# A hand-written TensorE order for the samples' attention, with pieces of gate products between a unit's parts and their weights issued from ScalarE's queue

## Chip, cores and metric

The kernel runs on one core of a Trainium2 chip. The metric is the device time of one execution in microseconds, taken as the median of several runs. TensorE is called PE, its weight load PEld, VectorE DVE, ScalarE ACT, GpSimd POOL and the sync engine SP. SP issues the DMAs of the kernel before, except for one kind that POOL issues.

## What is computed

One layer of a decoder is computed for a prompt of 512 tokens and for 8 samples of 8 tokens (64 token columns). The part that the change touches is the attention of the samples. It reads the cached latent rows in pages of 128 keys, and carries a running maximum, sum and accumulator over them.

```python
def step(carry, pid):
    m, l, acc = carry
    c = cache_kv_latent[layer, pid]
    kr = cache_k_rope[layer, pid]
    s = scores(c, kr)                       # q_abs . c + q_rope . kr, scaled
    m_new = jnp.maximum(m, jnp.max(s, -1))
    corr = jnp.exp(m - m_new)
    p = jnp.exp(s - m_new[..., None])
    acc = acc * corr[..., None] + jnp.einsum('bhtk,bkl->bhtl', p, c.astype(f32))
    return (m_new, l * corr + jnp.sum(p, -1), acc), None
```

Around it stand products that do not depend on this attention: the two gates `sigmoid(g_a)` and `sigmoid(g_c)`, which are parts of the input projection, the convolution's projection `w_oc`, and, for the prompt's columns, the attention's projection `w_oa`. They merge into `m = sigmoid(g_a) * y_a + sigmoid(g_c) * y_c`, which `w_o` projects. A layer norm and a feed-forward block follow.

## The kernel before

All rows stand transposed, with channels on the partitions and the 576 token columns in two halves of 288. A product is exact to fp32 by a split of both operands into a high and a low part: `mm3` (lines 116 to 119) makes three matmuls of it, named by lines 117, 118 and 119 in the profile. A weight tile comes by `wload` (line 98): a DMA into `wr` (line 107, three buffers), then `split` (line 56): ACT copies the high part to `wh` (line 57), and DVE subtracts it to give `wl` (line 60). `wh` and `wl` have three buffers of 512 columns each.

The program runs in stages: conditioning and first projections; the prompt's attention, with other products merged in; the samples' attention, with the gate products merged in; the output projection with the first norm; the feed-forward block with the second.

The samples' attention has 36 units: for each of 4 pairs of samples one unit of the step's own rows (64 keys) and 8 units of 4 pages for each sample of the pair. `load` (line 556) fetches a unit: SP reads 8 page numbers into registers (line 563) and issues 8 DMAs of 256 KB into `raw` (line 569), and POOL issues 4 indirect DMAs into `kr` (line 573). There are 7 places of `raw`, two to a unit, and 3 of `kr`. `scores` (lines 613 to 633) splits `kr` by ACT (`krh`) and DVE (`krx`, line 625), then multiplies the queries with the latent rows (line 630) and with the rotary rows (line 632). `values` (lines 635 to 680) takes the maximum on DVE (line 646), the exponential on ACT (`S`), transposes `S` on PE (line 653), copies it on ACT (`pT`), multiplies it with the pages on PE (line 661, `pv`), and adds to the accumulator on DVE (line 669). The last unit of a pair also transposes the accumulator (line 676).

The other products are a generator: `fill_gates` (8 tiles of one gate, 8 of `w_oc`, 8 of the other gate) and `fill_oa` (8 tiles of the merged branches). A gate tile is `dense` (line 309): 48 matmuls of 288 columns. `merge` (line 745) draws units of both generators in a ratio. Only SP keeps the written order in this stage. Elsewhere the recording layer's scheduler fixes each engine's order when the program is built, from its own estimate of when things are ready; on the chip every engine then runs its list in that order. As SP keeps the written order, the weights of a tile stand on SP's queue behind the page loads that were written before them, and a page load waits for a place of `raw` to come free.

Of the kernel before, what the change touches and what calls it, by code (L numbers as in the profile page):

```python
# [16 lines left out]
SEQ = 512  # L17
# [8 lines left out]
KVL = 256  # L26
# [17 lines left out]
# column offsets of the per-channel vectors  # L44
# [3 lines left out]
def build(tc, a):  # L48
# [40 lines left out]
    # ---------------------------------------------------------------- base  # L89
# [6 lines left out]
    # weight stream: pool, ring of split tiles, columns of a tile  # L96
    wp = [pool("w", side="right"), 3, 512, 3]

    def wload(src, n=1024, hl=None, tag="", to=None, eng=None):
        """a weight tile and its exact split, as a list of (hi, lo) pieces of wp[2] columns"""  # L100
# [3 lines left out]
        for c in range(0, n, step):  # L104
            m = min(step, n - c)
            raw = wp[0].tile([128, step], F32, tag="wr", bufs=wp[3], name="wr")
            dma(out=raw[:, :m], in_=src[:, c:c + m])
# [31 lines left out]
    def halves(t):  # L139
        """operands of a half-token tile [128, 2, K, HT]"""  # L140
# [8 lines left out]
    def rsqrt(p, vv, out, table=True):  # L149
        """out = 1/sqrt(vv): exp(-ln/2), then one Newton step"""  # L150
# [15 lines left out]
    # right-hand stack: what outlives the attention phases  # L166
# [19 lines left out]
    # ---------------------------------------------------------------- start: ada, h  # L186
# [31 lines left out]
    # weights of the conditioning, in part where results come later  # L218
# [5 lines left out]
    # a quarter of the conditioning gives a quarter of the modulated rows, and those a quarter of the first three tiles  # L224
# [48 lines left out]
    # ---------------------------------------------------------------- latent projections  # L273
    # on the right what the queries end with, on the left what the prompt's attention ends with
# [88 lines left out]
    # values of the prompt, token-major  # L363
# [9 lines left out]
    # new latent rows of the samples, token-major  # L373
# [17 lines left out]
    # ---------------------------------------------------------------- fillers  # L391
# [48 lines left out]

    def fill_gates():
        gc = gates["gc"]
        for j in range(8):
            dense(win(MT["gc"][0] + j), lambda ps, h_, sl: act(gc[:, j, sl], ps))
            yield 1
        act(gc, gc, AF.Sigmoid)
        for j2 in range(4):
            w = wload(a["w_oc"][j2])
# [6 lines left out]
            yield 1  # L455
        ga = gates["ga"] = YP.tile([128, 8, T], F32, tag="y", bufs=1, name="ga")
        for j in range(8):
            dense(win(MT["ga"][0] + j), lambda ps, h_, sl: act(ga[:, j, sl], ps))
            yield 1
        act(ga, ga, AF.Sigmoid)  # L460
        yield 1
# [34 lines left out]
    def prompt_units():  # L496
        for pr in range(4):
# [32 lines left out]
            for kb in range(4):  # L530
                n = SEQ - 128 * kb
                pts = []
                for o in range(2):
# [4 lines left out]
                    pts.append(A2b.tile([128, SEQ], F32, tag="pt", bufs=4, name="pt"))  # L538
                    act(pts[o][:, :n], pt[:, :n])
                # the two heads' columns of the array work side by side  # L540
# [16 lines left out]
    def load(pa, gg):  # L557
        """GP pages of the two batches, and their rotary rows"""
# [18 lines left out]
    def prepare(wk):  # L577
        """the samples' queries against latent rows, and the rotary ones"""
# [5 lines left out]
        # rotary queries against [hi, lo] rows of the first batch, then of the second: block-diagonal  # L584
# [607 lines left out]
```

## Time and profile before

| what | value |
|---|---|
| median of 3 runs | 1171.45 us (1170.65 to 1172.48) |
| span of the profiled execution, first to last instruction | 1174.0 us |
| mean granted PE clock | 0.974 |
| PE busy | 1091.8 us (93%) |
| DVE, ACT, POOL busy | 537.7, 431.7, 225.1 us |
| DMA | 190.07 MB, mean 162 GB/s |
| samples' attention, about 277 to 656 us of the span | 379 us |

Of the profiled execution the profile gives the span and no time beside it; the span lies 2.5 us (0.2%) over the median of the runs. The end of a matmul is modelled and matmuls are pipelined, so a busy PE is not a PE at its peak. What a matmul costs is read from the distance between the starts of matmuls that follow each other.

### The profile page before, as it was taken

Reading aid. Unit: us, or ns where it says so; the run is one execution under the profiler, and the core shown is the slowest. Engines: PE = TensorE matmul, PEld = TensorE weight load, DVE = VectorE, ACT = ScalarE, POOL = GpSimd, SP = SyncE. Lnnn points to the kernel's source line nnn. Section 1 sums busy time; section 2 is a strip of 40 time slices with the busy share of each in tenths; the row PEclk is TensorE's granted clock in tenths of the full one; section 3 lists DMA queues with packets and bytes.
Section 4 is the critical chain, followed back from the end, with each engine's and each line's share of the span. In section 5 each row is a group of like instructions: output and inputs, shape, how many; then the busy total and the mean of one; then the engine's idle time right before and its main releaser. Section 6 shows DMA issues by size and latency. Waiting matters only on the chain.

```text
span 1174.0 us, 19868 instructions
## 1 busy us (share of the span) xinstructions
PE 1091.8 (93%) x7646; PEld 931.6 (79%) x7646; DVE 537.7 (46%) x1059; ACT 431.7 (37%) x859; POOL 225.1 (19%) x232
## 2 busy tenths in 40 slices
PE   6889999998798899989999889899999999999994
PEld 5878787785466466556569889899999999999994
DVE  3476354443132333332247787933233333355656
ACT  2474343435232522332346355332223222334433
POOL 1120000023442342441301421800000000001303
PEclk9999999999799998999999899999999999999998
DMA  9626354418389586696675423032222222455551
GB/s 366 209 96 204 122 185 141 140 46 311 106 294 321 170 300 214 220 310 244 203 239 172 159 73 108 3 107 91 90 72 79 100 75 72 118 178 150 157 181 54
DMA packets 84941, 190.07 MB, mean 162 GB/s; under 512 B 11600, under 2 KB 15568, under 8 KB 84848
## 3 DMA queue, kind: packets, MB, share of 16 engines
q1 hardware_dynamic: 80752, 180.42, 45.8%
q0 software_dynamic: 4096, 8.40, 2.3%
q8 instruction: 60, 0.98, 0.3%
q14 instruction: 33, 0.27, 0.1%
HBM read 185.72 MB, written 3.06 MB: 161 GB/s over the span
## 4 chain that ended last, share of the span: by engine, by line
PE 48%; DVE 7%; DMA 5%; issue 2%; ACT 1%; SPq 1%; POOL 0%; POOLq 0%; ACTq 0%; DVEq 0%
PE acc L117 10%; PE acc L118 9%; PE acc L119 9%; PE sc L117 4%; PE sc L119 4%; PE sc L118 4%; PE sc L630 3%; DMA wr<-in_w_ff_dram 3%; PE pv L661 3%; DVE xr L60 2%; DVE wl L60 2%; ACT wh L57 1%; PE sc L632 1%; SPq L569 1%; DMA raw<-in_page_dram 1%
## 5 line engine op out<-in xcount | busy, mean ns | idle before, releaser
L117 PE MATMUL acc<-h,wl 128*128 128x288 f32 x960 | 288.7, 302 | 14.1 <-DVE wl L60 8.5
L118 PE MATMUL acc<-h,wh 128*128 128x288 f32 x960 | 286.9, 299 | 2.0 <-DVE h L60 1.5
L119 PE MATMUL acc<-h,wh 128*128 128x288 f32 x960 | 284.7, 297 | 1.9 <-issue 1.9
L60 DVE TENSOR_TENSOR wl<-wr,wh 128x512 fp32r<-128x512 f32 (+1 forms) x186 | 178.7, 966 | 212.1 <-ACT wh L57 206.1
L57 ACT ACTIVATE wh<-wr 128x512 fp32r<-128x512 f32 (+2 forms) x196 | 156.6, 807 | 194.5 <-DMA wr<-in_w_ff_dram 58.7
L117 PEld LDWEIGHTS acc<-h,wl 128*128 128x128 f32 x960 | 181.5, 189 | 25.9 <-DVE wl L60 11.2
L118 PEld LDWEIGHTS acc<-h,wh 128*128 128x128 f32 x960 | 182.2, 190 | 7.3 <-issue 5.0
L119 PEld LDWEIGHTS acc<-h,wh 128*128 128x128 f32 x960 | 182.6, 190 | 3.1 <-issue 2.9
L573 POOL DMA_INDIRECT kr<-in_krT_dram,idx x128 | 122.7, 959 | 227.4 <-ACT krh L57 103.0
L117 PE MATMUL sc<-h,wl 128*128 128x288 f32 x336 | 99.9, 297 | 0.0
L118 PE MATMUL sc<-h,wh 128*128 128x288 f32 x336 | 99.4, 296 | 0.0
L119 PE MATMUL sc<-h,wh 128*128 128x288 f32 x336 | 99.1, 295 | 0.0
L630 PE MATMUL sc<-raw,qa 128*64 128x512 f32 x256 | 85.3, 634 | 3.2 <-DMA raw<-in_page_dram 1.8
L60 POOL TENSOR_TENSOR xr<-xr,h 128x288 f32<-128x288 f32 x16 | 17.2, 1098 | 366.1 <-ACT h L57 362.5
L117 PE MATMUL acc<-f,wl 128*128 128x288 f32 x288 | 85.9, 298 | 1.6 <-DVE wl L60 1.6
L118 PE MATMUL acc<-f,wh 128*128 128x288 f32 x288 | 84.9, 295 | 0.0
L119 PE MATMUL acc<-f,wh 128*128 128x288 f32 x288 | 84.7, 294 | 0.0
L661 PE MATMUL pv<-raw,pT 128*64 128x256 f32 x512 | 68.8, 401 | 12.5 <-ACT pT L57 6.3
L661 PEld LDWEIGHTS pv<-raw,pT 128*64 128x64 f32 x512 | 38.5, 143 | 37.7 <-issue 16.0
L119 PEld LDWEIGHTS sc<-h,wh 128*128 128x128 f32 x336 | 63.6, 189 | 0.0
L118 PEld LDWEIGHTS sc<-h,wh 128*128 128x128 f32 x336 | 63.3, 189 | 0.1
L117 PEld LDWEIGHTS sc<-h,wl 128*128 128x128 f32 x336 | 63.2, 188 | 0.1
(326 smaller groups left out, 1767.1 us busy)
## 6 DMA issues: line engine op xcount, KB each, us to landing
raw<-in_page_dram SPq DMA_DIRECT2D x256, 256.0 KB
wr<-in_w_ff_dram SPq DMA_DIRECT2D x76, 512.0 KB
wa<-in_w_ada_dram SPq DMA_DIRECT2D x40, 512.0 KB
wr<-in_w_in_dram SPq DMA_DIRECT2D x64, 256.0 KB
wr<-in_w_ff_dram SPq DMA_DIRECT2D x16, 384.0 KB
wr<-in_w_o_dram SPq DMA_DIRECT2D x18, 256.0 KB
wr<-in_w_oa_dram SPq DMA_DIRECT2D x16, 256.0 KB
x<-in_xT_dram SPq DMA_DIRECT2D x4, 576.0 KB
```

Source lines behind the costliest of these rows:

```text
L57: nc.scalar.activation(out=out, in_=in_, func=func, **kw)
L60: return (eng or v).tensor_tensor(out=out, in0=in0, in1=in1, op=op)
L117: mm(ps, lhsT=wl, rhs=xh, start=start, stop=False)
L118: mm(ps, lhsT=wh, rhs=xl, start=False, stop=False)
L119: mm(ps, lhsT=wh, rhs=xh, start=False, stop=stop)
L569: dma(out=raw[:, j], in_=a["page"][bass.ds(vs[GP * e + j], 1)].rearrange("a p d -> p (a d)"))
L573: g.indirect_dma_start(kr[:, 128 * j:128 * j + 128], None, a["krT"], bass.IndirectOffsetOnAxis(ap=idx[:, i:i + 1], axis=0))
L630: mm(ps[rows(e), :n], lhsT=qa[:, c, 2 * pa + e], rhs=rhs, start=c == 0, stop=False)
L632: mm(ps[:, :n], lhsT=qr[:, i, pa].rearrange("p e q -> p (e q)"), rhs=kx, start=False, stop=i == 0)
L661: mm(pv[rows(e), :KVL], lhsT=pT[:np_, j, e], rhs=rhs, start=j == 0, stop=j == nj - 1)
```

## The change

`values` is cut in three. The maximum, the exponential and the sums move into `scores`; `turn` makes the transposes and `pT`; `values` keeps the products with the pages and the accumulator; `attended` transposes a finished accumulator one unit later. A piece of another product (half a gate tile, one tile of `w_oc` or of `w_oa`) is drawn by `fill` after the values of every unit, and in 8 of the 36 units a second one between the transposes and the scores. PE now keeps the written order in this stage, as SP does. The weights of these pieces are issued from ACT's queue (`wq`), no longer from SP's. In the prompt's attention the two heads' transposes are written in the other order. Comments and descriptions in the code are blank lines now.

```diff
-    def wload(src, n=1024, hl=None, tag="", to=None, eng=None):
+    def wload(src, n=1024, hl=None, tag="", to=None, eng=None, q=None):
...
-            dma(out=raw[:, :m], in_=src[:, c:c + m])
+            (q or dma)(out=raw[:, :m], in_=src[:, c:c + m])
...
+    wq = nc.scalar.dma_start
+
+    def dense_chunks(i, dst):
+        w = wload(a["w_in"][i - 3], q=wq)
+        pss = [ps_acc(), ps_acc()]
+        for p in range(2):
+            gpart(pss, w[p], hs, 0, range(4 * p, 4 * p + 4), 8)
+            if p:
+                for ps, sl in zip(pss, sls):
+                    act(dst[:, sl], ps[:, :HT])
+            yield 1
...
-            dense(win(MT["gc"][0] + j), lambda ps, h_, sl: act(gc[:, j, sl], ps))
-            yield 1
+            yield from dense_chunks(MT["gc"][0] + j, gc[:, j])
...
-                for o in range(2):
+                for o in (1, 0):
                     pt = ps_sc()
...
+            act(S[:, :n], (S if new else ps)[:, :n], AF.Exp, bias=nb[:, g1], scale=SCALE,
                 accum_out=(ll if new else ls)[:, g1])
+            if not new:
+                act(cx[:, g1], mx[:, g0], AF.Exp, bias=nb[:, g1], scale=SCALE)
...
+            return S
...
-            cur, nxt = nxt, scores(*units[i + 1], pages[i + 1]) if i + 1 < len(units) else None
-            values(*u, cur, pages[i])
-            yield 1
+            more = i + 1 < len(units)
+            if more:
+                kx = krn if units[i + 1][1] < 0 else rotary(pages[i + 1])
+            pT = turn(*u, S)
+            fill(2 * i)
+            if more:
+                S = scores(*units[i + 1], pages[i + 1], kx)
+            values(*u, pT, pages[i])
+            fill(2 * i + 1)
+            if u[1] < 0 and u[0] or not more:
+                attended(u[0] - 1 if more else u[0])
...
-            to_m(j, 0, woa(j), gates["a3"])
-            yield 0.25
-        wo.append(wload(a["w_o"][0]))
+            to_m(j, 0, woa(j, q=wq), gates["a3"])
+            yield 1
+        wo.append(wload(a["w_o"][0], q=wq))
...
-        merge(sample_units(A3, qa, qr, pages), F, 21 - PF - P3, 37)
+    A3 = gates["a3"] = pool("a3")
+    extra = 48 - 2 * PF - len(units)
+
+    def fill(s):
+        i = s // 2
+        if s % 2 or (i + 1) * extra // len(units) > i * extra // len(units):
+            next(F, None)
+    with tc.manual_schedule(engines={mybir.EngineType.SP, mybir.EngineType.PE}):
+        sample_stage(A3, qa, qr, pages, fill)
         for _ in F:
             pass
```

On PE, before, this stands in the third pair, where three units follow each other without other work. `raw` are pages, `qa` the queries, `S` the exponentials, `pT` their transposes; L630 and L632 are scores, L653 transposes, L661 values, L117 a gate piece.

```order
L630 MATMUL sc<-raw,qa 64x512
L661 MATMUL pv<-raw,pT 64x256 x8
L630 MATMUL sc<-raw,qa 64x512 x3
L632 MATMUL sc<-krx,qr 128x512 x2
L653 MATMUL sc<-ident,S 128x128 x4
L630 MATMUL sc<-raw,qa 64x512
L661 MATMUL pv<-raw,pT 64x256 x8
L653 MATMUL sc<-ident,S 128x128 x4
L630 MATMUL sc<-raw,qa 64x512 x3
L632 MATMUL sc<-krx,qr 128x512 x2
L661 MATMUL pv<-raw,pT 64x256 x8
L117 MATMUL acc<-h,wl 128x288
```

On PE, after the change, a unit of the first pair reads as follows; L670 is now the transposes, L644 and L646 the scores of the unit after it, L683 the values, and L117 to L119 begin a piece of 24 matmuls.

```order
L119 MATMUL acc<-h,wh 128x288
L670 MATMUL sc<-ident,S 128x128 x4
L644 MATMUL sc<-raw,qa 64x512 x4
L646 MATMUL sc<-krx,qr 128x512 x2
L683 MATMUL pv<-raw,pT 64x256 x8
L117 MATMUL acc<-h,wl 128x288
L118 MATMUL acc<-h,wh 128x288
```

Between a unit's scores and its transposes there now stand the values of the unit before and a whole piece; between its transposes and its values stand the scores of the next unit.

On ACT, before, in the first pair, `krh` is the rotary rows' high part of a later unit, `S,sm` the exponential, `sm` the correction, `gct` a gate tile's copy and `wh` two weight pieces.

```order
L57 ACTIVATE krh<-kr 128x512
L57 ACTIVATE S,sm<-sc,sm 128x512
L57 ACTIVATE sm<-sm 128x1
L57 ACTIVATE wh<-wr 128x512 x2
L57 ACTIVATE pT<-sc 128x512
L57 ACTIVATE krh<-kr 128x512
```

On ACT, after the change, at the same place in the program, the weights' DMAs stand in its list.

```order
L107 DMA wr<-in_w_in_dram 128x512
L57 ACTIVATE krh<-kr 128x512
L57 ACTIVATE S,sm<-sc,sm 128x512
L57 ACTIVATE sm<-sm 128x1
L57 ACTIVATE wh<-wr 128x512
L57 ACTIVATE pT<-sc 128x512
L107 DMA wr<-in_w_in_dram 128x512
```

One weight piece is split in a unit where there were two in every second, and one DMA is issued behind the copy of `pT`.

On SP, before, a gate tile's weights stand between the page loads of two units (L563 reads the page numbers, the ISA rows set an address).

```order
L569 DMA raw<-in_page_dram 128x512
L107 DMA wr<-in_w_in_dram 128x512 x2
L563 TENSOR_LOAD ptab
L569 ISA
L569 DMA raw<-in_page_dram 128x512
```

On SP, after the change, page loads follow page loads.

```order
L579 ISA
L579 DMA raw<-in_page_dram 128x512
L573 TENSOR_LOAD ptab
L579 ISA
L579 DMA raw<-in_page_dram 128x512
```

The two weight DMAs have left the place between them.

More of the change, by code (lines that the diff above doesn't have):

```diff
@@ L454, in fill_gates @@
                     tt(gc[:, j, sl], gc[:, j, sl], ps[:, :HT], MULT)
-            yield 1
+                yield 1
         ga = gates["ga"] = YP.tile([128, 8, T], F32, tag="y", bufs=1, name="ga")
         for j in range(8):
-            dense(win(MT["ga"][0] + j), lambda ps, h_, sl: act(ga[:, j, sl], ps))
-            yield 1
+            yield from dense_chunks(MT["ga"][0] + j, ga[:, j])
         act(ga, ga, AF.Sigmoid)
-        yield 1
     def fill_ada():
@@ L537, in prompt_units @@
                                             Ss[o][:, offs[i] + 128 * kb:offs[i] + 128 * kb + 128], ident)
-                    pts.append(A2b.tile([128, SEQ], F32, tag="pt", bufs=4, name="pt"))
+                    pts[o] = A2b.tile([128, SEQ], F32, tag="pt", bufs=4, name="pt")
                     act(pts[o][:, :n], pt[:, :n])
@@ L604, in prepare, with sample_stage @@
         return qa, qr
-    def sample_units(A3, qa, qr, pages):
+    def sample_stage(A3, qa, qr, pages, fill):
         smask = A3.tile([128, 4, NS], F32, name="smask")
@@ L611, in rows, with rotary, scores @@
             return slice(64 * e, 64 * e + 64)
-        def scores(pa, gg, pages):
+        def rotary(pages):
+            krh = A3.tile([128, GK], F32R, tag="krh", bufs=1, name="krh")
+            kx = A3.tile([128, GK], F32R, tag="krx", bufs=2, name="krx")
+            act(krh, pages["kr"])
+            v.scalar_tensor_tensor(out=kx, in0=krh.bitcast(F32), scalar=nm, in1=pages["kr"], op0=MULT, op1=ADD)
+            return kx
+        def scores(pa, gg, pages, kx):
             ps = ps_sc()
@@ L619, in scores @@
                 smt[pa] = A3.tile([128, 8, NG + 1], F32, tag="sm", bufs=2, name="sm")
-                kx = krn
-            else:
-                krh = A3.tile([128, GK], F32R, tag="krh", bufs=1, name="krh")
-                kx = A3.tile([128, GK], F32R, tag="krx", bufs=2, name="krx")
-                act(krh, pages["kr"])
-                v.scalar_tensor_tensor(out=kx, in0=krh.bitcast(F32), scalar=nm, in1=pages["kr"], op0=MULT, op1=ADD)
             for c in range(2):
@@ L632, in scores @@
                 mm(ps[:, :n], lhsT=qr[:, i, pa].rearrange("p e q -> p (e q)"), rhs=kx, start=False, stop=i == 0)
-            return ps
-        def values(pa, gg, ps, pages):
-            sm = smt[pa]
-            mx, gm, nb, ls, ll, cx = [sm[:, i] for i in range(6)]
+            mx, gm, nb, ls, ll, cx = [smt[pa][:, i] for i in range(6)]
             g0, g1 = slice(gg, gg + 1), slice(gg + 1, gg + 2)
-            new = gg < 0
-            k, np_, nj = (NS, NS, 1) if new else (GK, 128, GP)
             S = A3.tile([128, GK], F32, tag="S", bufs=2, name="S")
@@ L654, in values @@
             pT = A3.tile([128, GP, 2, NS], F32, tag="pT", bufs=2, name="pT")
-            src = pt[:np_, :128 * nj].rearrange("p (j e q) -> p j e q", j=nj, e=2)
-            act(pT[:np_, :nj], src)
+            act(pT[:np_, :nj], pt[:np_, :128 * nj].rearrange("p (j e q) -> p j e q", j=nj, e=2))
+            return pT
+        def values(pa, gg, pT, pages):
+            new = gg < 0
+            np_, nj = (NS, 1) if new else (128, GP)
+            g1 = slice(gg + 1, gg + 2)
             pv = ps_pv()
@@ L687, in sample_units @@
         smt, acct = {}, {}
-        nxt = scores(*units[0], pages[0])
+        S = scores(*units[0], pages[0], krn)
         for i, u in enumerate(units):
@@ L724, in to_m, with woa @@
         split(mf, M[h_][:, 0, j], M[h_][:, 1, j])
-    def woa(j, eng=None):
-        return wload(a["w_oa"][j // 2][:, 512 * (j % 2):512 * (j % 2) + 512], 512, eng=eng)
+    def woa(j, eng=None, q=None):
+        return wload(a["w_oa"][j // 2][:, 512 * (j % 2):512 * (j % 2) + 512], 512, eng=eng, q=q)
     def fill_oa():
@@ L768, in build @@
     with tc.manual_schedule(engines={mybir.EngineType.SP}):
-        for _ in range(PF):
+        for _ in range(2 * PF):
             next(F)
```

30 lines of the change are left out of this document (15 added, 15 removed).

## Prediction

> **What bounds the kernel now.** I read the page first, then the busy time by stage, the stage's groups and waits, and last the order in time.
>
> ```profile
> span 1174.0 us, 19868 instructions
> 120.00:277.00 157.00, 155.53 (x1085) 120.62 (x1085) 70.44 (x186) 64.16 (x163) 10.48 (x18) 1.00 0.41 138
> 277.00:310.00 33.00, 25.62 (x123) 15.41 (x123) 9.47 (x24) 10.79 (x26) 16.63 (x17) 0.79 0.50 178
> 310.00:630.00 320.00, 295.36 (x1830) 200.26 (x1826) 104.43 (x259) 110.37 (x241) 97.92 (x104) 0.97 0.72 244
> 630.00:656.00 26.00, 20.89 (x145) 19.83 (x144) 24.16 (x38) 10.49 (x24) 12.93 (x4) 0.92 0.54 183
> 330.00:370.00 40.00, 39.49 (x273) 29.79 (x269) 13.47 (x32) 13.70 (x32) 17.78 (x19) 1.00 0.88 298
> 370.00:410.00 40.00, 31.35 (x187) 18.38 (x186) 11.68 (x29) 17.42 (x31) 11.31 (x12) 0.96 0.65 218
> ```
>
> The columns are the stretch, its length, busy time of PE, PEld, DVE, ACT and POOL, the granted clock, the DMA share and GB/s. PE is the busiest in each; DVE and ACT are busy a third of the samples' stage (277 to 656). But PE is not full there: 330 to 370 has 39.49 us busy, 370 to 410 only 31.35. To see how much is lost I price the work by a stretch in which PE is fed, from start to start.
>
> ```profile
> 332.16 0.38 PE L117 MATMUL acc<-h,wl 128*128 128x288 f32 x1
> ...
> 338.73 1.95 PE L661 MATMUL pv<-raw,pT 128*64 128x256 f32 x16
> 340.50 1.89 PE L630 MATMUL sc<-raw,qa 128*64 128x512 f32 x8
> 342.32 0.73 PE L632 MATMUL sc<-krx,qr 128*128 128x512 f32 x2
> 342.89 0.60 PE L653 MATMUL sc<-ident,S 128*128 128x128 f32 x4
> 343.42 1.07 PE L630 MATMUL sc<-raw,qa 128*64 128x512 f32 x2
> ```
>
> From 332.16 to 338.73 run the 48 matmuls of a gate tile: 6.57 us, so 3.28 for a piece of 24 and 0.41 for each three. A unit of pages costs 1.77 (values) + 1.82 + 0.57 (scores) + 0.53 (transposes) = 4.69 us.
>
> ```profile
> L630 PE MATMUL sc<-raw,qa 128*64 128x512 f32 x256 | 85.3, 634 | 3.2 <-DMA raw<-in_page_dram 1.8 <-issue 1.4
> L117 PE MATMUL acc<-h,wl 128*128 128x288 f32 x249 | 77.0, 309 | 10.5 <-DVE wl L60 8.5 <-issue 1.8
> L117 PE MATMUL acc<-yt,wl 128*128 128x288 f32 x64 | 20.0, 312 | 0.3 <-issue 0.3
> L117 PE MATMUL acc<-oh,wl 128*128 128x288 f32 x32 | 9.6, 300 | 0.0
> ```
>
> These are the stage's groups (277 to 656), with the count behind the x and the idle time ahead of them last. 256 / 8 = 32 units of pages cost 150 us, 249 + 64 + 32 = 345 threes cost 141, and the 4 own-row units and the ends I estimate at a third of a page unit each and 4 us, 10 in all. That is 301 us of work in 379: **78 us are lost**, and the change can only win from these.
>
> ```profile
> PE pv L661 <- ACT pT L57: 6.3, 5, 3.1
> PE pv L661 <- issue: 6.1, 6, 2.4
> PE sc L653 <- issue: 3.5, 5, 1.0
> PE acc L119 <- issue: 3.4, 5, 1.0
> PE acc L117 <- issue: 2.2, 4, 1.1
> SPq L569 <- PE pv L661: 104.2, 18, 21.3
> ```
>
> These are waits of the stage (total, times, longest). Four parts can be read: the half clock, 33 x 0.21 + 320 x 0.03 + 26 x 0.08 = 18.6 us by the clock column; the rows with "issue", where PE waits for nothing that the profile shows, 15.2; weights, 8.5 (by the second row of the groups); `pT`, 6.3. The other 29 us lie in waits too short for rows, where transposes and values follow their inputs with no work between them.
>
> **The change, part by part.** PE's order: the products are the same in number, so it costs nothing by itself and is worth what it covers. A unit with a piece takes 4.69 + 3.28 = 7.97 us. The two chains beside it:
>
> ```profile
> L646 DVE TENSOR_REDUCE sm<-sc 128x1 f32<-128x512 f32 x32 | 22.1, 690 | 64.4 <-PE sc L632 54.3 <-issue 9.1 <-PE sc L653 1.0
> L625 DVE SCALAR_TENSOR_TENSOR krx<-krh,nm,kr 128x512 fp32r<-128x512 f32 x32 | 23.8, 744 | 1.7 <-ACT krh L57 1.3 <-issue 0.4
> L57 ACT ACTIVATE krh<-kr 128x512 fp32r<-128x512 f32 x32 | 20.1, 629 | 31.4 <-DVE sm L60 15.9 <-issue 13.3 <-DVE krx L625 2.3
> L57 ACT ACTIVATE S<-sc,sm 128x512 f32<-128x512 f32 x32 | 21.6, 676 | 4.2 <-DVE sm L648 3.3 <-DVE sm L60 0.6 <-issue 0.2
> L57 ACT ACTIVATE pT<-sc 128x512 f32<-128x512 f32 x32 | 19.1, 596 | 77.9 <-PE sc L653 53.3 <-remote 11.4 <-PE sc L632 5.5
> L57 ACT ACTIVATE wh<-wr 128x512 fp32r<-128x512 f32 x53 | 31.9, 623 | 24.4 <-DMA wr<-in_w_o_dram 10.2 <-DMA wr<-in_w_in_dram 9.5 <-DVE acc L669 2.3
> ```
>
> From scores to transposes: maximum 0.69, `krx` 0.74, `krh` 0.63 (it stands ahead of `S` on ACT), `S` 0.68, and some 0.5 for four hand-overs, in all 3.2 us, beside values and a piece, 1.77 + 3.28 = 5.05. It is covered by 1.8 us; with a `w_oa` piece, half as long, cover is 3.4. From transposes to values: `wh` 0.62 and `pT` 0.60 beside the scores, 2.4 us. ACT's list in a unit is `krh`, `S`, `wh`, `pT`, about 2.5 us, with the small ones and the copies 3.5 of 7.97. I charge 0.2 us a unit for misses, **7 us**; bounds 0 and 1 us a unit, 36.
>
> The two sigmoids over a whole gate break this:
>
> ```profile
> 619.60 1.28 ACT L57 ACT_TABLE_LOAD   x1
> 620.89 4.05 ACT L57 ACTIVATE ga<-ga 128x4608 f32<-128x4608 f32 x1
> ```
>
> The first will hold `pT` for 5.3 us beside 2.4 of scores; the second, with a table load behind it too, `S` for 6.6 beside 3.4. **6 us** are lost; between 0 and 12.
>
> The weights' queue: 44 loads of 256 KB leave SP for ACT.
>
> ```profile
> 324.39 0.84 SPq L107 DMA_DIRECT2D wr<-in_w_in_dram  x2
> 544.23 4.30 DMA wr<-in_w_in_dram
> 414.62 4.67 DMA kr<-in_krT_dram,idx
> ```
>
> On ACT one issue should take 0.42 us as on SP, within the 4 us that ACT has free. Behind an issue that waits stands all of ACT: the next `krh` and `S`, so PE's transposes. But a piece is asked for three pieces ahead, some 24 us, and lands in 4.3. SP gains: before, weights stood behind page loads that waited 104.2 us for values. Of the 8.5 us in which PE waits for weights, one wait of 4.5 is at the stage's end (its row is below) and stays; the other **4 us** go. Bounds: none of the 8.5 left, and 16 lost, twice as much.
>
> By the Trainium skill, "DMA: Bandwidth & Descriptors", section "Issuing engines are not separate DMA queues", moving an issue to another engine saves only the sequencer's time. By that rule the 4 us would stay lost, and the sum would be 1144. The trace speaks against it in so far as what SP loses here is no issue time but 104.2 us of waiting ahead of other issues.
>
> The stage's end: the 8 `w_oa` pieces go from the end into units, and so no longer cover the chain after the last values.
>
> ```profile
> 641.82 4.00 DVE wl L60 x2
> 642.26 12.93 POOL L796 TENSOR_SCALAR xr<-xr 128x1152 f32<-128x1152 f32 x4 [67.69 <-DMA xr<-in_xT_dram]
> 652.25 0.61 PE L117 MATMUL acc<-h,wl 128*128 128x288 f32 x1 [4.54 <-DVE wl L60]
> ```
>
> DVE's weight splits take 2 us each beside POOL's four rows, and that stays. 3 us more are lost there: **7.5** with the wait of 4.5.
>
> DMA: a unit moves 2.10 MB of pages, 0.26 of weights and 0.26 of rotary rows (4 x 128 x 128 values of 4 bytes), 2.62 MB in 7.97 us, 329 GB/s, though only 282 over 9 units with the own rows and the second pieces. 330 to 370 ran at 298 with PE full and a DMA share of 0.88, so about 338 at a share of 1. In the last pair, where half of the pieces are of `w_oa` and short, 22 MB in 67 us are 328 throughout, close to that: **4 us**, bounds 0 and 8.
>
> The rest: half clock 6 of 18.6, as its spells follow gaps that mostly go (0 to 18.6); issue waits 12 of 15.2 (8 to 18), as nothing in the order bears on them; the start, 277 to 310, 4 us (0 to 10). The prompt's attention has PE busy 155.53 of 157, so its other order of transposes is covered: 0, at most 2 either way.
>
> Left are 7 + 6 + 7.5 + 4 + 6 + 12 + 4 = 46.5 us of loss in place of 78: a gain of 31.5 us, and a span of 1142.5. The span of before is 2.5 us over the median of its runs, and the same gain on the median gives **1140 us**.
>
> **Rivals.** 1. The gaps go and the half clock and most issue waits go with them: 78 - 16 (8 for issue, 8 for the end) at the most, likely 45 to 50, **1124 us**. For it speaks that 330 to 370 has clock 1.00 and almost no gap in the kernel as it is; against it the issue waits, which I can't place. By the Trainium skill, "TensorE: Matmul & The Clock Gate", section "What's actually happening", an idle window of about 3.4 us halves the clock. The rows agree that it comes and goes with gaps (0.79 in the worst stretch, 1.00 in the full one), and by that rule alone the 6 us above would be 0 and the sum 1134.
>
> 2. Pages become the bound. PE's order is rigid, so a late page stops every product behind it. If the DMAs hold no more than 270 GB/s, 32 x 2.62 = 84 MB take 310 us, to which come the start and the end, 33 and 20, and 3 for the new end: 366 in place of 379, **1158 us**. Against it: 298 and more was held for 40 us.
>
> 3. ACT's list becomes the bound, and the kernel is slower. The place is `krh`, which stands ahead of `S` and waits for rotary rows loaded three units ahead.
>
> ```profile
> 309.37 0.94 POOL L573 DMA_INDIRECT kr<-in_krT_dram,idx  x1 [8.36 <-DVE sm L648]
> 310.62 0.94 POOL L573 DMA_INDIRECT kr<-in_krT_dram,idx  x1 [0.30 <-issue]
> ```
>
> POOL takes 1.25 us for each of 4, 5.0, and 4.67 to land: with the release some 11.4 us after its place is free, of 17.5 that two units and the chain give. It decides from 17.5 on. If it holds ACT 2 us over its cover in each of 32 units, 64 us come on top of the 46.5, which is 32.5 more than the 78: **1204 us**. From 1.0 us a unit on (31.5 / 32) nothing is won.
>
> 4. The order does what it says but PE was bound elsewhere, the gaps only move: **1171 us**. The 78 us speak against it.
>
> **How the numbers follow.** My forecast (1130 to 1152) gets 0.52, rival 1 (below 1130) 0.20, rival 2 (1152 to 1169) 0.14, rival 4 0.05, rival 3 0.09. The bounds of the terms together would reach from 1110 to 1205, but they don't come all at one end. The range 1119 to 1169 leaves out 0.05 of rival 1 and rivals 3 and 4, 0.19 in all. A measurement of this kernel can tell about 0.2% from no change: faster 0.86, same 0.05, slower 0.09.
>
> **What would show it.** The stage's length falls from 379 to about 348. Right: units with a piece repeat at about 8 us, SP's wait for values stays long, the row of `pT` as what PE waits for falls under 3 us, and the clock of 310 to 630 is at 0.98 or over. Wrong: PE waits for pages, `krx` or `S` in most units, DMA stays under 260 GB/s in the middle, or ACT waits in front of `krh` or a DMA issue.

## The result, and the profile after

The changed kernel takes **1153.56 us** (median of 4 runs, 1151.87 to 1156.49) against 1171.05 us for the kernel before: a ratio of 0.9852 with a 95% interval of 0.9834 to 0.9870, 17.5 us faster. Measured again with other runs the ratio was 0.9857 (0.9829 to 0.9886). The forecast was 1140 us, 31.5 us faster, in a range of 1119 to 1169.

The span of the profiled execution falls from 1174.0 to 1151.7 us. First the busy time by stretch of the changed kernel, in the columns of the prediction (the stretch, its length, busy PE, PEld, DVE, ACT and POOL, the granted clock, DMA share, GB/s).

```profile
span 1151.7 us, 19837 instructions
276.00:310.00 34.00, 21.56 (x120) 13.07 (x121) 7.11 (x18) 9.15 (x24) 19.47 (x20) 0.85 0.50 167
310.00:630.00 320.00, 300.97 (x1975) 212.09 (x1971) 132.24 (x296) 121.56 (x266) 107.83 (x104) 0.97 0.76 252
330.00:370.00 40.00, 37.87 (x260) 26.32 (x261) 13.27 (x34) 14.14 (x34) 15.09 (x16) 1.00 0.87 286
```

The stage now ends near 630. PE holds 300.97 us in the 320 us of its middle, where it held 295.36, but its start is no better than before: 21.56 of 34. To compare runs in which work stands in another order I measure the stage at the same work, from the first matmul of the own rows' scores to the 4050th of the 7646 matmuls, some way into the output projection. By that it takes 356.2 us where it took 382.0: in these two executions 25.8 us of the 31.5 were won. What stands behind it took 504.8 us against 500.6.

Next the stage's waits (total, times, longest; the first four are PE's, the last is SP's) and two of its groups (idle time ahead of them last).

```profile
PE pv L683 <- ACT pT L57: 17.9, 15, 7.6
PE sc L670 <- issue: 4.9, 2, 4.4
PE sc L670 <- ACT S L57: 4.2, 1, 4.2
PE acc L117 <- DVE wl L60: 3.5, 3, 1.7
SPq L579 <- PE pv L683: 141.8, 28, 21.7
L644 PE MATMUL sc<-raw,qa 128*64 128x512 f32 x256 | 64.6, 627 | 0.0
L117 PE MATMUL acc<-h,wl 128*128 128x288 f32 x248 | 77.9, 314 | 3.6 <-DVE wl L60 3.5
```

Pages never held PE up for long: its scores stood idle 0.0 us, and SP waits 141.8 us for values, more than before. The waits put down to "issue" have shrunk to 5.1 us (the 4.9 shown and one of 0.2). Before they were 19.8: beside the four rows of 15.2 us that the prediction added up, the same view has three more.

```profile
PE sc L632 <- issue: 2.1, 1, 2.1
PE sc L630 <- issue: 1.4, 1, 1.4
PE acc L118 <- issue: 1.1, 3, 0.4
```

What grew is the wait of the values for `pT`, 6.3 to 17.9 us. One of its 15 cases takes 7.6 us. Here are PE, ACT and POOL around it, in order of time; a row's end has the engine's idle time ahead of it and what ended that.

```profile
293.34 0.74 PE L646 MATMUL sc<-krx,qr 128*128 128x512 f32 x2
301.65 0.69 PE L683 MATMUL pv<-raw,pT 128*64 128x256 f32 x2 [7.56 <-ACT pT L57]
290.74 0.28 ACT L57 ACTIVATE sm<-sm 128x1 f32<-128x1 f32 x1
300.48 0.63 ACT L57 ACTIVATE wh<-wr 128x512 fp32r<-128x512 f32 x1 [9.46 <-remote]
301.02 0.58 ACT L57 ACTIVATE pT<-sc 128x512 f32<-128x512 f32 x1
290.89 0.94 POOL L583 DMA_INDIRECT kr<-in_krT_dram,idx  x1 [0.31 <-DMA kr<-in_krT_dram,idx]
...
297.13 0.94 POOL L583 DMA_INDIRECT kr<-in_krT_dram,idx  x1 [0.30 <-issue]
```

PE, ACT and DVE all stand still, and only POOL works. ACT's `wh` waits for the piece that frees its buffer, and PE's last matmul of that piece started at 290.08. By the trace's records of semaphore updates, PE's update for it came at 300.46, with three more of PE's within 0.2 us, and `wh` starts 0.02 us later. So the word of this work came 10 us late. The ends of matmuls are modelled, and no row says outright that the work itself was done by then. But PE's granted clock falls to half at 299.0 us, ahead of these updates and 4.9 us behind the start of this gap, as it does 3.5 to 4.4 us behind the start of the gaps that end at 270.7, 281.9 and 388.2. That speaks for a PE with nothing left to do. A usual unit shows the same in small, here with the transposes and values of PE and ACT's two copies.

```profile
346.19 0.60 PE L670 MATMUL sc<-ident,S 128*128 128x128 f32 x4
350.09 1.08 PE L683 MATMUL pv<-raw,pT 128*64 128x256 f32 x8 [0.77 <-ACT pT L57]
348.92 0.63 ACT L57 ACTIVATE wh<-wr 128x512 fp32r<-128x512 f32 x1 [4.94 <-PE sc L644]
349.45 0.58 ACT L57 ACTIVATE pT<-sc 128x512 f32<-128x512 f32 x1
```

The last matmul of the piece that `wh` waits for starts at 346.06, and `wh` starts at 348.92. So I took every instruction of PE that updates its semaphore, and the first update recorded at or behind its end, and called it late if over 0.3 us lay between. In the stretch from 277 to 640 us:

```
                     beside an indirect DMA of POOL     no indirect DMA
before               60 of  89 late                      7 of 129 late
changed              64 of 108 late                      9 of 154 late
```

These counts are too high, since an update whose record is missing counts as late. If the records are paired with the updates in order, each with the latest that fits, 26 of the 89 and 17 of the 108 have no record, and 37 and 52 are late, by up to 11.3 and 10.1 us. So paired, no update of ACT or DVE is late in this stretch of any trace, though beside indirect DMAs their records are missing too (54 of ACT's 101 and 66 of DVE's 100 in the kernel before). Where an engine's start follows the late update, as above, the lateness is real.

Ahead of this stretch 4 and 1 come late, behind it, where POOL issues no indirect DMA, none of about 190. This was my new theory: **PE's signals come late while POOL gathers rotary rows**, and that is what most of "issue" stood for in the profile of before. It speaks of both kernels, so it has to say how much of the change's gain is cover against it.

### The profile page after: what moved, and what is told of

Same layout as the page of the kernel before. It is cut to its first block, busy times and chain, and to the rows that moved or that the text cites. A ratio compares the mean times of both kernels' runs of the same rounds, so it can differ in the third digit from the quotient of the medians.

```text
span 1151.7 us, 19837 instructions
## 1 busy us (share of the span) xinstructions
PE 1066.9 (93%) x7646; PEld 920.0 (80%) x7646; DVE 542.7 (47%) x1059; ACT 432.5 (38%) x860; POOL 223.2 (19%) x232
## 4 chain that ended last, share of the span: by engine, by line
PE 76%; DVE 8%; DMA 6%; ACT 4%; issue 3%; another core or an unknown queue 2%; SPq 1%; POOL 0%; POOLq 0%; ACTq 0%; DVEq 0%
PE acc L117 15%; PE acc L118 14%; PE acc L119 14%; PE sc L117 6%; PE sc L118 5%; PE sc L119 5%; PE pv L683 5%; PE sc L644 5%; DMA wr<-in_w_ff_dram 4%; DVE xr L60 2%; DVE wl L60 2%; PE acc L198 2%; DMA raw<-in_page_dram 1%; ACT wh L57 1%
## 5 line engine op out<-in xcount | busy, mean ns | idle before, releaser
L60 DVE TENSOR_TENSOR wl<-wr,wh 128x512 fp32r<-128x512 f32 (+1 forms) x186 | 181.5, 978 | 265.5 <-ACT wh L57 228.7
L117 PE MATMUL acc<-h,wl 128*128 128x288 f32 x960 | 290.1, 303 | 10.5 <-DVE wl L60 4.9
L119 PE MATMUL acc<-h,wh 128*128 128x288 f32 x960 | 284.6, 297 | 0.0
L117 PEld LDWEIGHTS acc<-h,wl 128*128 128x128 f32 x960 | 181.6, 189 | 28.3 <-issue 11.8
L119 PEld LDWEIGHTS acc<-h,wh 128*128 128x128 f32 x960 | 182.1, 190 | 1.1 <-issue 0.8
L117 PE MATMUL sc<-h,wl 128*128 128x288 f32 x336 | 100.2, 298 | 0.0
L119 PE MATMUL sc<-h,wh 128*128 128x288 f32 x336 | 99.1, 295 | 0.0
L60 POOL TENSOR_TENSOR xr<-xr,h 128x288 f32<-128x288 f32 x16 | 16.8, 1072 | 369.9 <-ACT h L57 365.6
L117 PE MATMUL acc<-f,wl 128*128 128x288 f32 x288 | 85.8, 298 | 2.0 <-DVE wl L60 2.0
L119 PE MATMUL acc<-f,wh 128*128 128x288 f32 x288 | 84.8, 294 | 0.0
L683 PE MATMUL pv<-raw,pT 128*64 128x256 f32 x512 | 65.5, 400 | 18.0 <-ACT pT L57 17.9
L683 PEld LDWEIGHTS pv<-raw,pT 128*64 128x64 f32 x512 | 35.2, 142 | 45.0 <-ACT pT L57 24.4
L644 PE MATMUL sc<-raw,qa 128*64 128x512 f32 x256 | 64.6, 627 | 0.0
L117 PEld LDWEIGHTS sc<-h,wl 128*128 128x128 f32 x336 | 63.5, 189 | 0.1
L119 PEld LDWEIGHTS sc<-h,wh 128*128 128x128 f32 x336 | 63.5, 189 | 0.0
```

Of the source, the lines that this page charges most:

```text
L60: return (eng or v).tensor_tensor(out=out, in0=in0, in1=in1, op=op)
L117: mm(ps, lhsT=wl, rhs=xh, start=start, stop=False)
L119: mm(ps, lhsT=wh, rhs=xh, start=False, stop=stop)
L644: mm(ps[rows(e), :n], lhsT=qa[:, c, 2 * pa + e], rhs=rhs, start=c == 0, stop=False)
L683: mm(pv[rows(e), :KVL], lhsT=pT[:np_, j, e], rhs=rhs, start=j == 0, stop=j == nj - 1)
```

## The experiments

The kernels of one series ran on the same chip beside the kernel before: `e1` to `e4`; `c_after` and `e5` to `e7`; `e8` to `e10`; `e11`. Ratios are to the kernel before of the same series, with their 95% intervals.

**e1: the weights from SP's queue again.**

```diff
-    wq = nc.scalar.dma_start
+    wq = dma
```

> The change, but with the weights of the pieces issued from SP's queue again, in written order among the page loads. If the queue is worth what the prediction charges (4 us), or more because a weight now stands behind page loads that wait for values while PE's order is rigid: 1158 to 1175 us, and PE's rows that wait for wl grow from 4.9 us to 10 or more. Rival: ACT's list is held by its own DMA issues (one waited 3.7 us for the landing of a page just ahead of the prompt's last transposes), and SP had the time: 1146 to 1151 us, and the wait of 6.05 us of PE for pt at 264.7 us is gone.

1169.69 us, 0.9926 (0.9902 to 0.9951). Here are PE's two longest waits of its stage.

```profile
PE acc L117 <- DVE wl L60: 23.4, 11, 5.5
PE pv L683 <- ACT pT L57: 13.5, 9, 7.2
```

Waits for weights rise to 23.4 us, from 3.5 up to 630 us in the changed kernel and 4.9 with the stage's end. In the changed kernel the queue is worth 0.9926 - 0.9852, about 0.7% or 8 to 9 us. The rival fell, though ACT's list does pay for its DMA issues once: in the changed kernel one of them (269.67) waited for a page of SP's queue, and the prompt's last copies of `pt` behind it with it.

```profile
265.75 0.63 ACT L57 ACTIVATE wh<-wr 128x512 fp32r<-128x512 f32 x1 [2.25 <-DMA wr<-in_w_in_dram]
269.67 0.34 ACTq L107 DMA_DIRECT2D wr<-in_w_in_dram  x1
270.05 1.09 ACT L57 ACTIVATE pt<-sc 128x512 f32<-128x512 f32 x2 [3.67 <-DMA raw<-in_page_dram]
```

That issue waited on a semaphore which a page load of SP, issued at 261.59, also counted on; it landed at 269.59. PE stood still behind these copies:

```profile
270.70 0.90 PE L546 MATMUL sc<-ident,S 128*128 128x128 f32 x3 [6.05 <-ACT pt L57]
```

`c_after` and `e4` have the same stop, 5.4 and 5.1 us long. `e1` has none there, and its stage starts at 271.1 us, that of the changed kernel at 276.4. `e2` below, with ACT's queue and the first order of the transposes, has none either, but its stage starts at 281.1.

**e2 and e3: the order of the two heads' transposes**, taken out of the change, and put alone into the kernel before.

```diff
# e2, in the changed kernel
-                for o in (1, 0):
+                for o in (0, 1):
# e3, in the kernel before
-                for o in range(2):
+                for o in (1, 0):
```

> The change, but with the two heads' transposes of the prompt's attention written in the first order again. The prediction held this part for 0, at most 2 us: then 1152 to 1156 us. Rival: in the trace the changed kernel is 1.0 us ahead of the one before at its 840th matmul and 8.5 us ahead at its 1800th, all of it in the prompt's attention, where nothing else was changed; if that comes from this order, then 1159 to 1163 us.

> The kernel before with only the two heads' transposes of the prompt's attention written in the other order. By the prediction 1169 to 1173 us. By the rival (this order gives the 7 us that the changed kernel is ahead by the end of the prompt's attention): 1162 to 1166 us.

`e2`: 1164.00 us, 0.9882 (0.9844 to 0.9920), which overlaps with the change's 0.9834 to 0.9870, so it settles nothing. `e3`: 1176.71 us, 1.0011 (0.9979 to 1.0043): alone it is worth nothing. The trace of `e3` shows why. It reaches its 1800th matmul at 243.7 us, the kernel before at 251.3, for the transposes' order also changes what the scheduler puts around them; but then its stage takes 388.0 us where that of before took 382.0. What is won ahead of the stage is given back in it. That its start hangs on loads, which come no earlier, is my reading and not shown.

**e4 and e6: rotary rows without POOL**, in the changed kernel and in the kernel before. The gather is left out: one plain DMA a unit brings as many bytes from fixed rows.

```diff
-        for j in range(GP):
-            i = pa * NPAGES + GP * gg + j
-            g.indirect_dma_start(kr[:, 128 * j:128 * j + 128], None, a["krT"],
-                                 bass.IndirectOffsetOnAxis(ap=idx[:, i:i + 1], axis=0))
+        r0 = 512 * (pa * NG + gg) % 8192
+        dma(out=kr.rearrange("p (j d) -> p j d", j=GP), in_=a["krT"][r0:r0 + 512].rearrange("(j p) d -> p j d", p=128))
```

> The change, but with the rotary rows of a unit loaded by one plain DMA on SP's queue from fixed rows of the cache instead of four indirect ones on POOL: the gather is left out, the bytes are the same. In the trace of the changed kernel PE's semaphore updates come late (up to 10 us) in 64 of 108 cases while POOL runs an indirect DMA, in 9 of over 500 without. If the indirect DMAs cause that, and with it the stop of 7.6 us at 293.7 us and a part of the waits for pT: late updates are gone and the time is 1135 to 1147 us. Rival: the lateness lies only in the records, or follows the DMA traffic as such: 1151 to 1156 us, and the stop at 293.7 us stays.

> The kernel before with the rotary rows loaded by one plain DMA a unit from fixed rows, the gather left out, as it was done to the changed kernel (0.9641 against the kernel before there, with late updates of PE gone). If PE's waits that the profile puts down to nothing (issue, 15.2 us) and the half clock of the first units come from POOL's indirect DMAs: 1145 to 1158 us. Rival: only a rigid order suffers from them, the scheduler's order has other work ready: 1166 to 1173 us.

`e4`: 1134.98 us, 0.9641 (0.9606 to 0.9675). `e6`: 1145.76 us, 0.9782 (0.9753 to 0.9810), where the kernels beside it had late updates and it had hardly any (9 of 222, the longest 0.43 us); `e4` had none. Both rivals fell. The stretch 277 to 310 of `e4`, and its waits of PE in the stage:

```profile
277.00:310.00 33.00, 29.29 (x180) 18.20 (x179) 10.38 (x25) 11.37 (x28) 0.00 (x0) 0.95 0.80 266
PE sc L668 <- ACT S L57: 7.7, 4, 3.7
PE acc L117 <- DVE wl L60: 5.9, 2, 4.1
PE pv L681 <- ACT pT L57: 4.3, 1, 4.3
```

and the place of the 7.6 us stop, where values now follow scores at once:

```profile
293.04 0.73 PE L644 MATMUL sc<-krx,qr 128*128 128x512 f32 x2
293.71 1.52 PE L681 MATMUL pv<-raw,pT 128*64 128x256 f32 x12
```

The stage, measured at the same work in the profiled executions, takes 348.9 us in `e6` and 337.8 in `e4`. With gathers it took 382.0 and 356.2, 33 and 18 us more. By that, some 15 of the 25.8 us that the change wins there are cover against late signals and 11 its own. This split is an estimate from four single executions of three series, and the times of the runs don't settle it: by medians the gathers cost 24.3 us in the kernel before (1170.04 to 1145.76) and 18.6 in the changed one (1153.56 to 1134.98, in two series), which leaves 10.8 of the 17.5 us as the change's own; by ratios to the kernel before they cost both the same, 2.2% and 2.1% (0.9641 against 0.9852), and then nothing of the gain is cover. **What is shown is that the gathers cost either kernel about 2%, and that the late updates go with them.**

**c_after: the change once more, beside e5 to e7.**

> The change itself once more, on the chip of the next three runs, so that they can be compared with it: 0.983 to 0.987 of the kernel before, as in the first measurement. If the 17 us were of one chip only, the ratio differs.

1154.59 us, 0.9857 (0.9829 to 0.9886), as expected.

**e5: whole gate tiles**, so that half of the units have no piece behind their values. The edit also moves the second pieces of 8 units from between transposes and scores to behind the values.

```diff
     def fill(s):
         i = s // 2
-        if s % 2 or (i + 1) * extra // len(units) > i * extra // len(units):
+        if s % 2 == 0:
+            return
+        for _ in range(2 * (i % 2) + ((i + 1) * extra // len(units) > i * extra // len(units))):
             next(F, None)
```

> The change, but with whole gate tiles: two pieces behind the values of every second unit and none behind the others; everything else, the second pieces too, stays. This takes away half of the cover between scores and transposes (3.2 us of chain beside 1.8 of values alone). If the pieces between a unit's parts are what the change wins by: 16 units lose 1.4 us and more, 22 us and some half clock with it, 1175 to 1185 us (no better than the kernel before). Rival: the fixed order as such and the weights' queue bring the gain, and pieces need not stand in every unit: 1153 to 1160 us.

1166.76 us, 0.9961 (0.9939 to 0.9983). The wait that the prediction named is there:

```profile
PE sc L670 <- ACT S L57: 16.8, 12, 5.3
```

Transposes wait for `S` 16.8 us, 4.2 in the changed kernel; a unit without a piece mostly stands idle for 0.89 us at this place in the trace, where 1.4 was expected. Of the 15.5 us between the medians of `c_after` and the kernel before 12.2 go. The order is worth little without a piece in every unit, though what the moved second pieces have in this was not measured apart; the expectation named the mechanism and put the time about 8 us too high.

**e7: each rotary row gathered once.** Four indirect DMAs of 64 rows in place of 128; VectorE writes the low parts to the other 64 partitions.

```diff
-            act(krh, pages["kr"])
-            v.scalar_tensor_tensor(out=kx, in0=krh.bitcast(F32), scalar=nm, in1=pages["kr"], op0=MULT, op1=ADD)
+            act(kx[:64], pages["kr"])
+            tt(kx[64:], pages["kr"], kx[:64].bitcast(F32), SUB)
...
-                                 bass.IndirectOffsetOnAxis(ap=idx[:, i:i + 1], axis=0))
+                                 bass.IndirectOffsetOnAxis(ap=idx[:64, i:i + 1], axis=0))
...
```

> The change, computing the same, but each rotary row is gathered once and not twice: 64 rows in an indirect DMA instead of 128, the low part written by VectorE to the other 64 partitions. The DMAs are as many as in the change, with half of the rows. If the price goes with the rows that POOL writes, half of what the plain load won (25 us of 1171) is won: 1138 to 1145 us, and an indirect DMA takes clearly less than 0.94 us on POOL. Rival: it goes with the number of indirect DMAs: 1150 to 1155 us, and one still takes 0.94 us.

1168.99 us, 0.9983 (0.9963 to 1.0004): slower than the change, by more than either theory said. An indirect DMA takes hardly less on POOL (the mean duration in ns stands behind the busy time; the first row is of `e7`, the second of the changed kernel):

```profile
L583 POOL DMA_INDIRECT kr<-in_krT_dram,idx x120 | 108.8, 907 | 206.0 <-DVE sm L60 147.6 <-issue 28.3 <-ACT oh L57 23.8
L583 POOL DMA_INDIRECT kr<-in_krT_dram,idx x120 | 114.5, 955 | 193.2 <-ACT krh L57 132.2 <-issue 31.1 <-PE pv L553 22.4
```

and 64 of 101 updates beside them come late, as before. Half of the rows buy nothing. Of its span's 10.8 us over that of `c_after`, 7.0 lie behind the last packet of the output (8.6 us from there to the end, 1.6 in `c_after`); why is open.

**e8, e9, e11: two gathers a unit, and no sigmoid over a whole gate.** In `e8` and `e11` (one kernel) an indirect DMA brings 128 different rows, those of a unit's first two pages of each sample to partitions 0 to 63, those of the last two to 64 to 127. `e9` also replaces the sigmoids.

```diff
# e8, e11
-        for j in range(GP):
-            i = pa * NPAGES + GP * gg + j
+        for j in range(2):
+            i = 2 * (pa * NG + gg) + j
...
+            for r, r2, c in ((slice(0, 64), slice(64, 128), slice(0, GK // 2)),
+                             (slice(64, 128), slice(0, 64), slice(GK // 2, GK))):
+                act(kx[r, c], pages["kr"][r])
+                tt(kx[r2, c], pages["kr"][r], kx[r, c].bitcast(F32), SUB)
...
# e9 besides
-                    act(dst[:, sl], ps[:, :HT])
+                    act(dst[:, sl], ps[:, :HT], AF.Exp, scale=-1.0)
+                v.tensor_scalar(out=dst, in0=dst, scalar1=1.0, scalar2=None, op0=ADD)
+                v.reciprocal(out=dst, in_=dst)
...
```

> The change, computing the same, with two indirect DMAs of 128 different rows in a unit instead of four in which every row comes twice: the pages of a unit's first half go to partitions 0 to 63, those of its second half to 64 to 127, and ScalarE writes the high parts in place while VectorE writes the low parts to the other half. If the price goes with the number of indirect DMAs (64 rows instead of 128 in each won nothing), half of the 25 us that the plain load won are won: 0.972 to 0.978 of the kernel before, 1138 to 1145 us, and the stop of 8 us in the first units shrinks to 4 or less. Rival: the price goes with the transfers' arrival or with something else that the plain load changed: 0.983 to 0.988.

> The same, and the two sigmoids over a whole gate are replaced: each gate tile is copied from PSUM as exp(-x), and VectorE adds 1 and takes the reciprocal, tile by tile. The two stops of 4.1 and 4.4 us at the sigmoids (the prediction charged 6 us for them) and the half clock behind them should go, against 16 more pairs of operations on VectorE, which is busy 41% of this stage: 8 to 12 us less than with the paired gather alone. Rival: the gaps only move to the next wait, or VectorE's longer list delays the maximum: within 3 us of it.

> The paired gather once more. In its first measurement the kernel before took 1144.6 us and no update of PE came late even beside four indirect DMAs a unit, while in all measurements ahead of that it took 1170 to 1177 us and 55 to 64 updates came late. If the updates come late again here (the kernel before at 1165 us and more) and the price goes with the number of indirect DMAs: 0.972 to 0.978 of the kernel before, under the 0.9855 of the change; if it does not go with their number: 0.983 to 0.988. If no update comes late here: 0.993 to 0.997 of a kernel before at 1141 to 1150 us, as in the first measurement.

`e8`: 1138.82 us, 0.9948 (0.9929 to 0.9967). `e9`: 1138.09 us, 0.9942 (0.9921 to 0.9962). `e11`: 1138.27 us, 0.9944 (0.9923 to 0.9965). The surprise is the kernel before, which took 1144.63 us beside `e8` and `e9` and 1144.74 beside `e11`, and 1170 to 1177 in the earlier series, on one occasion on the same chip ten minutes before. In these two series no update came late in any kernel that was traced (`e8` to `e11`), and no record of PE is missing. A usual unit of `e8`, to be laid beside that of the changed kernel above:

```profile
330.34 1.95 PE L686 MATMUL pv<-raw,pT 128*64 128x256 f32 x16
335.52 0.60 PE L673 MATMUL sc<-ident,S 128*128 128x128 f32 x4
338.58 0.65 PE L686 MATMUL pv<-raw,pT 128*64 128x256 f32 x4
335.72 0.63 ACT L57 ACTIVATE wh<-wr 128x512 fp32r<-128x512 f32 x1 [2.31 <-PE acc L119]
336.26 0.58 ACT L57 ACTIVATE pT<-sc 128x512 f32<-128x512 f32 x1
```

`wh` starts 0.2 us behind the piece's end, values follow scores with no gap, and the next values start 8.24 us after these. With nothing late there was nothing for fewer gathers to win, so `e8` and `e11` can't tell whether the price goes with the number of indirect DMAs: that stays open. `e9` is no faster than `e8` (the intervals lie on each other), so the rival holds: its stage is 340.2 us against 340.5, and its transposes wait 13.3 us for `S` where those of `e8` wait 7.9.

**e10: the queue alone, in the kernel before.**

```diff
-            dense(win(MT["gc"][0] + j), lambda ps, h_, sl: act(gc[:, j, sl], ps))
+            dense(wload(a["w_in"][MT["gc"][0] + j - 3], q=nc.scalar.dma_start), lambda ps, h_, sl: act(gc[:, j, sl], ps))
...
-            w = wload(a["w_oc"][j2])
+            w = wload(a["w_oc"][j2], q=nc.scalar.dma_start)
...
```

> The kernel before, in the scheduler's order and with whole gate tiles, with only the weights of the gates, of w_oc, w_oa and the first w_o tile issued from ScalarE's queue. By the prediction's term 4 us of PE's waits for weights go: 1165 to 1169 us against 1170. By what the undone queue cost the changed kernel (0.9926 against 0.9855, 8 us) the queue is worth as much here: 1160 to 1164 us. Rival: the queue only pays where PE's order is rigid, since the scheduler placed other products in front of a late weight: 1168 to 1172 us.

1144.68 us, 1.0002 (0.9985 to 1.0020): nothing. That is the rival, in a series without late signals. `e1` was measured where signals were late, so whether the order or the lateness makes the queue worth something is not separated. The scheduler's order moved with the queue, too: 2047 matmuls stand ahead of the own rows' scores in `e10`, 1947 in the kernel before. Its trace, of the old order with four gathers a unit, has the last word on those: the start of the stage, and PE's longest wait in it.

```profile
277.00:310.00 33.00, 33.00 (x189) 21.75 (x188) 8.89 (x20) 13.67 (x34) 12.14 (x13) 1.00 0.70 237
PE acc L117 <- DVE wl L60: 7.3, 3, 5.7
```

PE is busy in all of the 33 us of which the profile of before had 25.62 with the clock at 0.79, and none of 113 updates beside an indirect DMA is late. Part of this is other work, as the own rows' scores start at 288.9 us there and at 276.8 before. `e6`, without gathers, starts them at 276.3, and its row lies between the two:

```profile
277.00:310.00 33.00, 30.61 (x190) 21.23 (x188) 10.48 (x26) 11.45 (x28) 0.00 (x0) 0.95 0.71 239
```

By the first way of counting, PE's late signals were, per series:

```
series                        kernel before   late of those beside an indirect DMA
first measurement             1171.05 us      60 of 89 (before), 64 of 108 (changed)
e1 to e4                      1177.00 us      55 of 87 (e1), 71 of 106 (e2), 55 of 90 (e3)
c_after, e5 to e7             1170.04 us      60 of 102 (c_after), 47 of 78 (e5), 64 of 101 (e7)
e8 to e10                     1144.63 us      0 of 32 (e8), 0 of 41 (e9), 0 of 113 (e10)
e11                           1144.74 us      0 of 31
```

Where signals are late the kernel before takes 1170 us or more; without gathers (`e6`, 1145.76 us) and in series where they are not late (1144.7; traced there were the kernels beside it) it takes the same. So in the kernel before the gathers' own time is hidden, and what costs goes with the lateness.

## Why the prediction came out as it did

**The direction was right, the mechanism in part.** The change wins from the stage's lost time, by pieces between the parts of every unit (`e5` takes 12.2 of 15.5 us away by moving them). The chains were read rightly: transposes wait for `S` once 4.2 us, at a sigmoid, and a unit with a piece repeats at 8.24 us where nothing is late (16 of 19 such units of `e8` lie at 8.22 to 8.24), against 7.97 and 0.2 for misses. What the prediction did not know is that a large part of the lost time was late signals. It expected 3.2 us of gain from the waits called issue and 28.3 from the rest; by the estimate above 15 came from late signals and 11 from the rest. That the two came out as near to the forecast as they did is in part luck.

Of the signs that the prediction named, SP's long wait for values is there (141.8 us). The row of `pT` was to fall under 3 us and rose to 17.9, the clock of 310 to 630 is 0.97 where 0.98 was named, and units with a piece repeat at 8.67 us where about 8 was. The DMAs moved 252 GB/s in the middle, under the 260 that was to speak for pages as the bound, and yet PE waited for no page: that sign was badly chosen.

**The size was off, 17.5 us for 31.5.** Of the 14.0 us that are missing, 5.7 lie in the stage (25.8 for 31.5), 3.5 ahead of it and behind it, and 4.8 in the profiled execution of before, which was not a usual one (see below).

**The term for the issue waits and the start had the wrong cause.** I called those waits "what I can't place", added up 15.2 us of 19.8, charged 12 as staying and 4 us for the start, and took the rest of the stage to be free of them. They were the visible part of late signals, which cost the kernel before 33 us in its profiled execution and 24 by the medians. What I left out is that a rigid order meets them too: 18 us of its stage, in two forms. The start holds a stop of 7.6 us; and a unit takes a median of 8.67 us, 0.43 over that of `e8`, as signals late by 1 to 2.6 us go past the cover between transposes and values, 2.4 us beside a chain of 1.2. The other stop at the start, of 4.4 us (`issue` for L670), is not one of them, though with it the start has 12.0 us of stops for the 4 charged: it stays where nothing is late, as transposes that wait for the first `S` (the first row is of the changed kernel, the second of `e4`).

```profile
281.89 0.41 PE L670 MATMUL sc<-ident,S 128*64 128x128 f32 x1 [4.36 <-issue]
282.33 0.42 PE L668 MATMUL sc<-ident,S 128*64 128x128 f32 x1 [3.71 <-ACT S L57]
```

**The other terms.** The sigmoids were charged 6 us and cost 4.0 and 4.2:

```profile
383.60 4.04 ACT L57 ACTIVATE gct<-gct 128x4608 f32<-128x4608 f32 x1
388.18 1.12 PE L683 MATMUL pv<-raw,pT 128*64 128x256 f32 x4 [4.01 <-ACT pT L57]
```

but taking them out won nothing in `e9`, where 16 pairs of operations on VectorE stand in their place. The half clock should have left 6 of 18.6 us; by the same reckoning 34 x 0.15 + 320 x 0.03 = 14.7 are left, as its spells follow gaps that did not go. By the Trainium skill, "TensorE: Matmul & The Clock Gate", section "What's actually happening", such a spell follows an idle window of about 3.4 us; the trace agrees, with a spell that begins at 299.0 us behind the stop at 294.1, and in the 33 us of `e10` without a gap the clock is 1.00. The pages were charged 4 us and cost none. The stage's end was charged 7.5 us, with one wait of 4.5; in its place stand four waits for weights of at most 1.7 us, 4.9 in all, between 617 and 631.

**The weights' queue was mispriced, both ways.** I took 4 us from SP's 104.2 us of waiting. In the order of before it is worth nothing (`e10`, 1.0002), as the rule of the Trainium skill weighed in the prediction says ("DMA: Bandwidth & Descriptors", section "Issuing engines are not separate DMA queues"). In the changed kernel it is worth 8 to 9 us (`e1`). That fits a PE that can't pass a late weight, but as signals were late in the one series and not in the other, the rigid order is not shown to be the reason. ACT's list paid 3.67 us once for the queue, at 270.05, and PE 6.05 us with it, for which the prediction had no term. The other order of the prompt's transposes was charged 0 and is worth 0 alone (`e3`).

**The profiled execution was not a usual one.** A run of the changed kernel is its span and 1.8 us (1153.45 for 1151.7). By that the profiled execution of before took 1175.8 us, 4.7 over its median, where I reckoned with 2.5. Of the 22.3 us by which the spans differ 17.5 are left between the medians.

**The rivals.** Pages as the bound: no wait of PE for them. ACT's list: one stop, ahead of the stage, not 32. Gaps that only move: so it was at the sigmoids, in `e9`. The first, that gaps, half clock and issue waits go together, was right in what belongs together: in the order of before all three mostly go where nothing is late (`e10`). That the change would take them away was wrong.

**What stays open.** Why signals are late in three series and not in two, and whether POOL's issuing or the transfers behind it make them late. Each run on record has a recorded span and clock, so whether the recording has a part in it can't be told either. Open are also whether fewer gathers help where they are late, and what the change is worth where they are not, since it was not run there. From `e4` and `e6` it would be 0.9641 / 0.9782 = 0.986 by their ratios and 1134.98 / 1145.76 = 0.991 by their times; the two differ because the kernel before took 1177.00 us in the one series and 1170.04 in the other. The paired gather, which holds the whole change, beats the kernel before by 0.5 to 0.6% there (`e8`, `e11`); against the change itself it was not measured.

## What to carry to other kernels

An idle time that a profile puts down to nothing is not a constant: see which engine works through it, and take that engine's work out in one run before pricing it as staying. In this kernel a fixed order paid where each unit holds independent work longer than its chains, in every unit and not on average (`e5`). It also needed its weights fetched by a queue that waits for little else; in the scheduler's order, with no signal late, the same queue was worth nothing. Where a trace lacks records, pair them in order before calling one late. And lay the time of the profiled execution beside the runs before a sum is read from it.

## What the runs showed of the hardware

PE's semaphore updates can come late while POOL issues indirect DMAs: by up to 10 us (290.08 to 300.46) in a run of such DMAs, by 1 to 2.6 us beside four of them. It costs 2% of this kernel (`e6`, 0.9782), does not go down with the rows of a DMA (907 ns and 58 of 101 late for 64 rows, 955 ns and 52 of 108 for 128, with the records paired in order), and was there in three series and wholly absent in the four traces of two others, one of them on a chip that had shown it. By the same records ACT's and DVE's updates were not late. A DMA issue on ACT's queue can wait for the landing of a page that SP issued 8 us earlier, where both count on one semaphore.
